# A 16-run, 8 KB load whose data nobody uses, issued ahead of the first load of a relu-and-mean kernel

## The chip, the cores and the metric

One Trainium2 chip, one of its cores. The metric is the device time of one execution in microseconds (us), as a median over the executions of a kernel. The profile's span (first to last instruction) is about 1.35 us shorter than the time of the same execution: 160.2 and 161.59 us for the profiled execution before.

## The reference

```python
x: (32, 512, 1024) float32
def reference(x):
    return np.mean(np.maximum(x, 0), axis=-1).astype(np.float32)   # (32, 512)
```

16,384 rows of 1,024 numbers are read, 67.1 MB, and 64 KB are written.

## The kernel before

128 rows (called the "row", because each of the 128 partitions, the parallel lanes of the on-chip buffer, gets one of them) are handled on their own; the other 16,256 rows lie on 128 partitions, 127 each, and are loaded 16 at a time (8 MB, 64 KB per partition) into three buffers. Rows are shared out between ScalarE (relu with a sum) and VectorE (max and add with a sum). The last 15 rows come in smaller pieces. All loads are issued by the sync engine (SP). Two of them, the row and the first big load, are moved ahead of the barrier at which all engines meet at the start of the program.

```python
NB, BUFS = 16, 3
def load(i, dst, src):
    nc.sync.dma_start(out=dst, in_=src).then_inc(loaded[i], 16)

for t in range(full):                      # full = 7
    buf_free(t)                            # from t = 3: waits for both compute engines
    if t == 0:
        load(-1, row0[:, :], xfirst)       # the row: 128 runs of 4 KB
    load(t, bufs[t % BUFS][:, :, :], xr[:, t * NB:(t + 1) * NB, :])   # big: 128 runs of 64 KB
    if t == BUFS:
        nc.sync.wait_ge(first, 2)
        nc.sync.dma_start(out=..., in_=turned0[0:P:32, :]).then_inc(stored, 16)   # the row's result
# ... smaller loads of the last 15 rows ...
# ... reductions, mostly hidden behind the loads ...
nc.sync.wait_ge(pool, 2)
nc.sync.wait_ge(dve, n_done + 2)
nc.sync.dma_start(out=outr, in_=res[:, :]).then_inc(stored, 16)       # the final store
nc.sync.sem_clear(range(used[0], used[-1] + 1))
nc.sync.wait_ge(stored, 32).then_inc(stored, -32)
# ...
issue_ahead_of_entry_barrier(nc, 2)        # the first two loads go in front of the barrier
```

## Time and profile before

| | before |
|---|---|
| time, median of 4 runs | 161.47 us (161.30 to 161.62) |
| span of the profiled execution | 160.2 us |
| DMA queue, share of 16 engines' span | 97.7% |
| VectorE, ScalarE busy | 46%, 44% |
| first packet on a DMA engine | 1.03 us |
| big loads on the engines from | 2.75 us |
| last data landed, final store issued | 157.82, 158.57 us |

The time is that of the DMA stream. The prediction below shows the lines; two things help in reading them. In a table of stretches a packet counts where it starts, so a stretch in which sixteen long packets start shows far more than the true rate and the next ones show zero. And the issue of a DMA (an SPq line of the timeline) is the time in which the sync engine prepares it, not the time in which data moves.

### The profile page before, as it was taken

How to read it: one execution, taken by the hardware profiler on the slowest of the kernel's cores; microseconds unless marked ns; L12 is line 12 of the kernel's file. 1: busy time of each engine (PE TensorE's matmuls, PEld its weight loads, DVE VectorE, ACT ScalarE, POOL GpSimd, SP SyncE). 2: the span in 40 equal slices, each digit the busy share in tenths (PEclk: the TensorE clock that was granted, in tenths of full speed). 3: DMA queues.
4: the chain of work that ended last, by engine and by line, in shares of the span. 5: the costliest groups of instructions: out<-in, count | busy, mean ns of one | idle time of the engine just before them, and what ended most of it. 6: DMA issues, size and time to landing. Idle time of an engine off the chain costs nothing. (4 is left out here: it accounts for less than half of the span.)

```text
span 160.2 us, 347 instructions
## 1 busy us (share of the span) xinstructions
DVE 73.3 (46%) x131; ACT 70.4 (44%) x133; POOL 1.3 (1%) x9
## 2 busy tenths in 40 slices
DVE  0000029900498006960079500993009920299984
ACT  1400029800496006950079300991009900299983
POOL 1000000000000000000000000000000000000001
DMA  9969969979989899699699699699699797998992
GB/s 393 507 278 523 507 278 523 442 344 523 409 376 523 360 425 524 294 491 523 262 524 523 262 523 524 262 523 523 262 524 458 327 523 327 425 451 367 419 412 102
DMA packets 2312, 67.18 MB, mean 419 GB/s; under 512 B 392, under 2 KB 648, under 8 KB 1032
## 3 DMA queue, kind: packets, MB, share of 16 engines
q1 hardware_dynamic: 2312, 67.18, 97.7%
HBM read 67.11 MB, written 0.07 MB: 419 GB/s over the span
## 5 line engine op out<-in xcount | busy, mean ns | idle before, releaser
L20 DVE TENSOR_SCALAR_CACHE_REDUCE rows<-rows 128x1024 f32<-128x1024 f32 (+1 forms) x63 | 72.1, 1208 | 78.9 <-DMA rows<-in_x_dram 78.7
L15 ACT ACTIVATE rows<-rows 128x1024 f32<-128x1024 f32 x64 | 66.2, 1035 | 84.1 <-DMA rows<-in_x_dram 83.9
L15 ACT ACTIVATION_READ_ACCUMULATOR rows<-rows 128x1 f32 x64 | 11.9, 186 | 0.0
L20 DVE DVE_READ_ACCUMULATOR rows<-rows 128x1 f32 x63 | 5.2, 82 | 0.0
L168 DVE STREAM_TRANSPOSE turned<-mean 128x32 f32<-128x32 f32 x1 | 0.2, 213 | 5.9 <-ACT row L164 5.9
L164 ACT ACT_TABLE_LOAD x1 | 1.3, 1283 | 3.3 <-DMA row<-in_x_dram 3.3
L157 POOL TENSOR_SCALAR res<-sums 128x112 f32<-128x112 f32 (+1 forms) x2 | 0.5, 250 | 154.0 <-DVE rows L20 154.0
L164 ACT ACTIVATE row<-row 128x1024 f32<-128x1024 f32 x1 | 1.1, 1056 | 0.0
L15 ACT ACTIVATE last<-last 128x512 f32<-128x512 f32 x1 | 0.6, 630 | 0.0
L20 DVE TENSOR_SCALAR_CACHE_REDUCE last<-last 128x256 f32<-128x256 f32 x1 | 0.4, 420 | 0.3 <-DMA last<-in_x_dram 0.3
L197 DVE SCALAR_TENSOR_TENSOR last<-last,scale 128x258 f32<-128x258 f32 x1 | 0.4, 428 | 0.1
L142 POOL MEMSET scale<- 128x258 f32 x1 | 0.3, 314 | 0.0
L187 POOL TENSOR_SCALAR res<-part 128x1 f32<-128x1 f32 x1 | 0.3, 267 | 0.6 <-DVE rows L20 0.6
L164 ACT ACTIVATION_READ_ACCUMULATOR row<-row 128x1 f32 x1 | 0.2, 186 | 0.0
L15 ACT ACTIVATION_READ_ACCUMULATOR last<-last 128x1 f32 x1 | 0.2, 186 | 0.0
L141 POOL MEMSET mean<- 128x32 f32 x1 | 0.1, 126 | 1.5 <-POOLq L55 1.5
L232 POOL MEMSET const-uint8-127<- 128x1 uint8 x1 | 0.1, 103 | 0.0
L232 POOL MEMSET const-bfloat16-1.0<- 128x1 bf16 x1 | 0.1, 102 | 0.0
L232 POOL MEMSET const-float32-0.0<- 128x1 f32 x1 | 0.1, 99 | 0.2 <-issue 0.2
L232 POOL MEMSET const-float32-1.0<- 128x1 f32 x1 | 0.1, 99 | 0.0
L20 DVE DVE_READ_ACCUMULATOR last<-last 128x1 f32 x1 | 0.1, 83 | 0.0
L197 DVE DVE_READ_ACCUMULATOR last<-last,scale 128x1 f32 x1 | 0.1, 82 | 0.0
## 6 DMA issues: line engine op xcount, KB each, us to landing
rows<-in_x_dram SPq DMA_DIRECT2D x1, 3584.0 KB, 38.1
rows<-in_x_dram SPq DMA_DIRECT2D x1, 2048.0 KB, 42.6
rows<-in_x_dram SPq DMA_DIRECT2D x1, 1024.0 KB, 44.7
row<-in_x_dram SPq DMA_DIRECT2D x1, 512.0 KB, 3.3
rows<-in_x_dram SPq DMA_DIRECT2D x1, 512.0 KB, 45.4
last<-in_x_dram SPq DMA_DIRECT2D x1, 256.0 KB, 45.6
last<-in_x_dram SPq DMA_DIRECT2D x2, 128.0 KB, 45.4
rows<-in_x_dram SPq DMA_DIRECT2D x7, 48.8
```

What stands on the lines that cost most here:

```text
L15: return nc.scalar.activation(out=src, in_=src, func=ACT.Relu, accum_out=acc)
L20: return nc.vector.tensor_scalar(out=src, in0=src, scalar1=0.0, scalar2=init, op0=ALU.max, op1=ALU.add, accum_out=acc,)
L141: nc.gpsimd.memset(mean0[:, :], 0.0)
L142: nc.gpsimd.memset(scale[:, :], inv).then_inc(pool, 1)
L157: nc.gpsimd.tensor_scalar(out=res[:, lo:hi], in0=sums[:, lo:hi], scalar1=inv, scalar2=0.0, op0=ALU.mult, op1=ALU.add,)
L164: nc.scalar.activation(out=row0[:, :], in_=row0[:, :], func=ACT.Relu, scale=inv, accum_out=mean0[:, 0:1],).then_inc(first, 1)
L168: nc.vector.transpose(turned0[:, :], mean0[:, :]).then_inc(first, 1)
L187: nc.gpsimd.tensor_scalar(out=res[:, J - 2:J - 1], in0=part[:, 0:1], scalar1=part[:, 1:2], scalar2=inv, op0=ALU.add, op1=ALU.mult,).then_i ...
L197: nc.vector.scalar_tensor_tensor(out=last[:, 768:], in0=last[:, 768:], scalar=0.0, in1=scale[:, :], op0=ALU.max, op1=ALU.mult, accum_out=r ...
L232: nc = _bacc.Bacc("TRN2", target_bir_lowering=False, num_devices=1)
```

## The change

The probe asks what one more transfer costs when it stands in front of everything else. Its data (16 runs of 512 B, one for each DMA engine) goes to a buffer that nobody reads. A semaphore tells that it has landed, and the sync engine waits for it much later, ahead of the fourth big load.

```diff
     first = nc.alloc_semaphore("first")
+    probe, probed = sbuf("probe", 16, 128), nc.alloc_semaphore("probed")
@@
     for t in range(full):
         buf_free(t)
+        if t == BUFS:
+            nc.sync.wait_ge(probed, 16)
         if t == 0:
+            nc.sync.dma_start(out=probe[:, :], in_=xfirst[0:P:8, :128]).then_inc(probed, 16)
             load(-1, row0[:, :], xfirst)
@@
-    used = [s.num for s in (*loaded, act, dve, pool, first)]
+    used = [s.num for s in (*loaded, act, dve, pool, first, probed)]
@@
-    issue_ahead_of_entry_barrier(nc, 2)
+    issue_ahead_of_entry_barrier(nc, 3)
```

## The prediction

> **What bounds the kernel now.** I read the page first (busy shares, the 40 slices, the DMA queue, the groups of instructions), then the two views of waits (the engines' and the sync queue's own), then the timeline of the sync queue, and last a table of stretches that I cut finely around the first and the last transfer, because the change touches only the first microseconds.
>
> The page:
>
> ```profile
> span 160.2 us, 347 instructions
> DVE 73.3 (46%) x131; ACT 70.4 (44%) x133; POOL 1.3 (1%) x9
> ...
> DMA  9969969979989899699699699699699797998992
> ...
> q1 hardware_dynamic: 2312, 67.18, 97.7%
> HBM read 67.11 MB, written 0.07 MB: 419 GB/s over the span
> ```
>
> Both compute engines are busy under half of the span, and the one DMA queue holds 97.7% of sixteen engines' time. So it is a stream of 67 MB with reductions hidden behind it.
>
> The views of waits, the engines' first and the sync queue's below it:
>
> ```profile
> ACT rows L15 <- DMA rows<-in_x_dram: 83.9, 9, 17.2
> DVE rows L20 <- DMA rows<-in_x_dram: 78.7, 8, 16.9
> ...
> SPq L115 <- DVE rows L20: 104.6, 5, 29.5
> ```
>
> The engines wait for data, never for each other in the main part. The 104.6 us of the sync queue look like the opposite, loads held up because buffers are not free; they are not a loss. The sync queue asks for the buffer of the first big load at 32.28 us, when the second load has still some ten microseconds to go (it lands 48.8 us after issue in the median of the page's issue list) and the third is queued behind it. Two loads are always ahead of the DMA engines.
>
> The table of stretches (columns: stretch and length; busy time of VectorE, ScalarE, GpSimd; clock; DMA share; GB/s):
>
> ```profile
> 0.50:1.00 0.50, 0.00 (x0) 0.00 (x0) 0.00 (x0) 1.00 0.00 0
> 1.00:1.20 0.20, 0.00 (x0) 0.00 (x0) 0.00 (x0) 1.00 1.20 123
> 1.20:1.40 0.20, 0.00 (x0) 0.00 (x0) 0.00 (x0) 1.00 1.19 205
> 1.40:1.60 0.20, 0.00 (x0) 0.00 (x0) 0.00 (x0) 1.00 0.00 0
> 1.60:1.70 0.10, 0.00 (x0) 0.00 (x0) 0.00 (x0) 1.00 1.19 492
> 1.70:2.20 0.50, 0.00 (x0) 0.00 (x0) 0.27 (x2) 1.00 1.04 410
> ...
> 2.70:22.00 19.30, 0.21 (x1) 2.43 (x3) 0.00 (x0) 1.00 1.01 435
> ...
> 157.20:157.40 0.20, 0.05 (x2) 0.20 (x1) 0.00 (x0) 1.00 0.17 51
> 157.40:158.57 1.17, 0.86 (x4) 0.49 (x2) 0.27 (x1) 1.00 0.00 0
> ```
>
> A packet is booked in the stretch where it starts, so zeros between 1.4 and 1.6 us mean that every DMA engine was inside its first packet, not that it idled. The reader should see three parts: about 1.03 us with no packet, a start-up in which each engine takes until about 1.65 us over one 4 KB packet (the raw packet records give 0.25 to 0.66 us for these, 0.159 us for each after them), then a gapless stream at about 435 GB/s until 157.4 us, and a fixed tail of 2.8 us (last reductions, the store, its landing). The end is therefore the moment at which the stream gets going, plus bytes over rate, plus the tail. A change moves the end only through one of these three.
>
> **What the Trainium skill says, and whether the trace agrees.** The page "DMA: Bandwidth & Descriptors", section "Latency and other measured facts", puts the first byte of a DMA issued by the sync queue at about 600 ns. Here the first packet starts 1.03 us after its issue begins, which is 0.64 us after the issue instruction ends (0.39 us); taken from the end of the issue the two agree. The store at the end shows 0.85 us from the start of the issue, 0.50 from its end.
>
> The same page, section "Queues, rings and completion order", says that on each DMA engine descriptors are consumed in ring order. So the row load's packets stand behind the probe's on the same engines. This trace agrees: the first load's packets all precede those of the second, and the small store that was issued at 32.66 us moves its packets only at 80.2 us, behind the loads that were queued before it.
>
> Its section "Why a DMA increments its semaphore by 16 and not by 1" says that a transfer is split over the largest number of engines up to 16 that divides its slowest dimension. For 16 partitions that is 16: one run of 512 B on each engine. No run shows that shape yet.
>
> "Perfetto Trace Analysis", section "DMA Instruction — HWDGE (DVE, Sync)", says that the slice of an issue covers the generation of descriptors and not the movement of data. The trace agrees: the first issue ends at 0.39 us and its data is moving from 1.03 us.
>
> **The change part by part.** It removes nothing. It adds one DMA issue at the head of the sync queue, 16 runs of 512 B, one more semaphore, one more wait on the sync queue before the fourth big load, and one more number in the clearing of semaphores. The order of instructions on the other engines is unchanged.
>
> The issue. The timeline of the sync queue:
>
> ```profile
> 0.00 0.39 SPq L109 DMA_DIRECT2D row<-in_x_dram  x1
> ...
> 32.66 0.63 SPq L125 DMA_DIRECT2D out_dram<-turned  x1
> ...
> 158.57 0.35 SPq L205 DMA_DIRECT2D out_dram<-res  x1
> ```
>
> The issue time hardly follows the number of runs: 0.39 us for 128 runs of 4 KB, 0.35 for 128 of 508 B, 0.63 for 4 runs of 128 B, 0.33 to 0.44 for the big loads. So I take 0.33 to 0.44 us for the probe and 0.05 us of gap (0.39 to 0.45 in the timeline): the row load's issue begins 0.38 to 0.49 us later, say 0.43.
>
> The bytes. 8 KB over 16 engines is one packet of 512 B each. Runs of 508 B took 0.027 us in the store, runs of 1 KB 0.046 us in the last loads, and a semaphore write 0.009 us. So 0.04 to 0.06 us of each engine's time.
>
> The wait before the fourth load. The probe has landed some 30 us earlier, so it costs one passed wait, about 0.02 to 0.05 us, in a place with about ten microseconds of slack: 0 on the path. The longer clearing lies beside the landing of the final store: 0. The barrier at entry moves by the 0.43 us, since the sync queue reaches it last (its drain begins at 0.93 us), and the third and fourth loads are issued that much later. They are queued behind a load that runs to 22 us: 0.
>
> What reaches the end is only the delay of the stream. If the row's data keeps its distance from its issue, that is 0.43 us. But the start-up of 0.25 to 0.66 us on the first packet looks partly like a cost of the first access; if the probe takes it, its packets being on the engines by 1.03 us as the row's were, the row could run from about 1.65 us as now, and only the 0.05 us of the bytes remains. I weigh 0.43 at 60%, something between (0.2 to 0.3) at 25% and 0.05 at 15%: 0.26 + 0.06 + 0.01 = about 0.33 us. 161.53 + 0.33 = about 161.85 us.
>
> **The rivals.** First, the warm-up in full. For it: the four earliest packets took 0.656 us each and the late starters 0.25 to 0.3, so all end within a short time of each other, as if one common event released them. Against it: that event can as well be the end of the row load's own descriptor generation or its own first read of memory, which come later with the row. The time would be 161.55 to 161.6.
>
> Second, the row's packets stall behind the probe: the engine finishes the probe's semaphore write, with its wait for the data to be confirmed, before it reads on. For it: small transfers pay a latency of their own (the row's landing is told 0.35 us after its last packet). Against it: at the seam between the row and the first big load the semaphore write lasts 0.009 us and the next packet starts 0.006 us after its start. The time would be 162.1 to 162.3.
>
> Third, the shift is absorbed by slack downstream. It can't be: with two loads queued at every moment, nothing later makes the DMA engines catch up; they already run at 435 GB/s.
>
> Fourth, the extra small transfer shifts the engines' phase and changes the rate. 1% of 155 us would be 1.5 us, but each engine gets the same extra run, so I give it 3%.
>
> **Range and chances.** The shift should be 0.05 to 0.5 us and the three times of the kernel before spread over 0.3 us, so a median is good to some 0.1 to 0.15. That gives 161.45 to 162.2 for 8 in 10. A change of 2% is 3.2 us, seven times the largest term; I leave 1% for each side: 1% faster, 98% within 2%, 1% slower.
>
> **What would show it.** In the changed profile the timeline of the sync queue should show the probe's issue at 0.00 with 0.33 to 0.44 us and the row's at about 0.43. The stretches should show 8 KB of packets near 1.03 us; the row's pipelined packets should start near 2.05 us if the shift is full, near 1.7 us if the start-up is absorbed, and the first reduction of a big load should move from 22.98 to 23.4 or 23.03 accordingly. The stream's rate and the tail should be as before. I am wrong if the first big load's landing moves by over 0.6 us, or not at all or to the left, or if the end moves by a different amount than that landing.

## The result, and the profile after

| | before | after |
|---|---|---|
| time, median of 4 runs | 161.47 us (161.30 to 161.62) | 162.09 us (162.07 to 162.33) |
| ratio after over before | | 1.0040, 95% interval 1.0025 to 1.0055 |

A ratio is the mean time of one kernel's runs over that of the other's of the same rounds, so it is not quite the ratio of the medians. Executions over 1.5% slower than the fastest of the same kernel are left out of the means. The medians are 0.62 us apart; the interval stands for 0.40 to 0.89 us. By the 2% measure the two are the same; the order of the two is clear of the noise.

The page after, its busy shares, DMA row and queue:

```profile
span 161.0 us, 348 instructions
DVE 73.3 (46%) x131; ACT 70.4 (44%) x133; POOL 1.3 (1%) x9
...
DMA  9899799699699699699699699699898998899992
...
q1 hardware_dynamic: 2344, 67.18, 97.4%
```

Nothing in the middle has changed: the same busy times, and the queue's 97.4% of 161.0 us is as much busy time as the 97.7% of 160.2 us before, within 0.3 us. The 32 packets more are 16 of data and 16 semaphore writes, one of each for every DMA engine, as the prediction had it.

The timeline of the sync queue after (start, length, both in us):

```profile
0.00 0.40 SPq L124 DMA_DIRECT2D probe<-in_x_dram  x1
...
0.45 0.41 SPq L110 DMA_DIRECT2D row<-in_x_dram  x1
0.90 0.43 SPq L110 DMA_DIRECT2D rows<-in_x_dram  x1
...
159.19 0.35 SPq L210 DMA_DIRECT2D out_dram<-res  x1
```

The probe takes one slot, 0.45 us, and the row and the big load are issued that much later. The final store's issue moves from 158.57 to 159.19 us, 0.62 us, more than the slot. The table of stretches after:

```profile
1.00:1.20 0.20, 0.00 (x0) 0.00 (x0) 0.00 (x0) 1.00 0.12 31
1.20:1.40 0.20, 0.00 (x0) 0.00 (x0) 0.00 (x0) 1.00 0.03 5
1.40:1.60 0.20, 0.00 (x0) 0.00 (x0) 0.00 (x0) 1.00 0.68 189
```

At 1.0 us, where the row's 4 KB packets started before (123 and 205 GB/s in the first two stretches), there is now only the 8 KB of the probe; its packets take 0.025 us each. The row's first packet starts at 1.48 us, 1.03 us after its issue, exactly the distance before. The long first packets come later as well: in the packet records, the row's packets of over 0.3 us end between 1.65 and 1.81 us before and between 2.05 and 2.17 us after. Then two waits, before and after, from the view of the engines' waits (total, times, longest):

```profile
ACT L164 <- DMA row<-in_x_dram: 3.3, 1, 3.3
```

```profile
ACT L169 <- DMA row<-in_x_dram: 3.7, 1, 3.7
```

The row lands about 0.4 us later (0.35 us by the semaphore records). The first big load follows; its first reduction, in the timelines before and after:

```profile
22.98 1.06 ACT L15 ACTIVATE rows<-rows 128x1024 f32<-128x1024 f32 x1 [17.19 <-DMA rows<-in_x_dram]
```

```profile
23.52 1.06 ACT L15 ACTIVATE rows<-rows 128x1024 f32<-128x1024 f32 x1 [17.38 <-DMA rows<-in_x_dram]
```

That is 0.54 us. One more wait has changed, the sync engine's own for its final store, before and after, from the sync queue's view of waits:

```profile
SPq L210 <- SPq L210: 1.2, 1, 1.2
```

```profile
SPq L215 <- SPq L215: 1.3, 1, 1.3
```

The raw semaphore records give this more finely: from the store's last packet to its last semaphore arrival it is 0.44 us before and 0.56 us after. Each of the sixteen DMA engines sends one arrival: the first seven come within 0.34 us before and 0.29 us after, the other nine between 0.39 and 0.44 us before and between 0.51 and 0.56 us after. So the profiled execution after is longer in two places: the last data lands 0.64 us later, and the store is confirmed 0.12 us later. Their sum of 0.76 us is the difference between the two profiled executions, 162.33 and 161.59 us, within 0.02.

### The profile page after: what moved, and what is told of

The parts are those of the page before. It is cut to its first block, busy times and chain, and to the rows that moved or that the text cites. A ratio compares the mean times of both kernels' runs of the same rounds, so it can differ in the third digit from the quotient of the medians.

```text
span 161.0 us, 348 instructions
## 1 busy us (share of the span) xinstructions
DVE 73.3 (46%) x131; ACT 70.4 (44%) x133; POOL 1.3 (1%) x9
## 3 DMA queue, kind: packets, MB, share of 16 engines
q1 hardware_dynamic: 2344, 67.18, 97.4%
```

## The experiments

All twelve give correct results. Each ran in five rounds (4 to 6 executions that count) beside the kernel before on the same chip; diffs are against the changed kernel and cut to the lines that matter (the size of the probe's buffer, for one, is left out). Theory I: the sync queue's issue slot ahead of the first data is what costs. Rival B: bytes, semaphore, wait or later barrier cost, wherever the probe stands.

This table has, for the profiled execution of each, when the row's last part landed, when the sixteen DMA engines started their first packet of the first big load, when the last data landed, and how long the final store took from its last packet to its last confirmation (all from the packet and semaphore records, in us). "Sum" is the shift of the last landing plus that of the confirmation, against before; "profiled" is the difference of the two profiled executions' times. The last two columns are the timed runs: difference of the medians of the same rounds, and the ratio with its interval.

| kernel | row landed | big load's first packets | last landing | confirmed | sum | profiled | medians | ratio |
|---|---|---|---|---|---|---|---|---|
| before | 3.28 | 2.75 to 2.92 | 157.82 | 0.44 | | | | |
| the change | 3.63 | 2.87 to 3.45 | 158.46 | 0.56 | 0.76 | 0.74 | 0.62 | 1.0040 (1.0025 to 1.0055) |
| e1 the change again | 3.80 | 3.09 to 3.49 | 158.25 | 0.56 | 0.55 | 0.53 | 0.53 | 1.0032 (1.0019 to 1.0046) |
| e12 4 runs ahead | 3.62 | 2.80 to 3.54 | 157.96 | 0.58 | 0.27 | 0.29 | 0.55 | 1.0030 (1.0016 to 1.0045) |
| e9 128 runs ahead | 3.67 | 3.04 to 3.43 | 158.21 | 0.91 | 0.86 | 0.83 | 1.03 | 1.0060 (1.0045 to 1.0075) |
| e4 two ahead | 4.15 | 3.50 to 3.80 | 158.89 | 1.19 | 1.81 | 1.80 | 1.29 | 1.0080 (1.0067 to 1.0094) |
| e8 a whole row ahead | 4.63 | 3.97 to 4.78 | 159.84 | 1.01 | 2.59 | 2.55 | 2.72 | 1.0152 (1.0129 to 1.0175) |
| e5 no probe | 3.21 | 2.36 to 3.16 | 157.62 | 0.45 | -0.19 | -0.21 | 0.06 | 1.0003 (0.9984 to 1.0022) |
| e6 behind the big load | 3.52 | 2.67 to 3.10 | 157.87 | 0.58 | 0.19 | 0.17 | 0.32 | 1.0013 (0.9996 to 1.0030) |
| e3 ScalarE's queue | 3.35 | 2.53 to 2.98 | 157.68 | 0.56 | -0.02 | -0.01 | 0.13 | 1.0017 (1.0004 to 1.0031) |
| e2 behind the row | 3.34 | 2.73 to 4.71 | 160.06 | 0.57 | 2.37 | 2.36 | 2.52 | 1.0158 (1.0144 to 1.0172) |
| e7 128 runs behind the row | 3.26 | 3.59 to 5.53 | 159.89 | 0.75 | 2.38 | 2.35 | 2.83 | 1.0173 (1.0147 to 1.0198) |
| e10 128 runs of 8 B behind | 3.26 | 2.69 to 5.28 | 160.02 | 0.87 | 2.62 | 2.59 | 2.80 | 1.0169 (1.0150 to 1.0188) |
| e11 as e7, big load later | 3.31 | 2.99 to 4.05 | 158.90 | 0.99 | 1.63 | 1.61 | 1.81 | 1.0108 (1.0092 to 1.0125) |

Two checks before the table is used. "Sum" and "profiled" agree within 0.04 us in every row, so the two terms are the whole account: nothing else in the program has changed its length. And single profiles of equal kernels differ: the last landing is 0.20 us earlier in e5 than before, where nothing should differ. The four kernels with one transfer ahead lie further apart, from 157.96 to 158.46 us. So some tenths of a microsecond of one last landing are noise, and means over several kernels or the timed runs must carry small claims. The profiles also come from different chips, and the one of the kernel before was taken apart from the experiments'; e5 to e8 share a chip and their rounds.

### e1: the change again

No edit.

> The changed kernel again, to narrow its cost. Theory I (the sync queue's issue slot): one issue plus gap is 0.45 us in the profile (0.00 to 0.45), so 0.40 to 0.50 us over before, ratio 1.0028. Theory L (landing): the row's packets also start later or slower behind the probe, as the last landing moved by 0.64 us in the one profile: 0.60 to 0.70 us, ratio 1.004.

Measured: ratio 1.0032, that is 0.52 us (0.31 to 0.74). With the first four runs (0.40 to 0.89) the cost lies near 0.55 to 0.6 us. Both intervals hold both expectations, so neither run decides between 0.45 and 0.62. Its profile does name the parts: 0.43 us in the last landing, 0.12 us in the confirmation of the store, again.

### e2: the probe second, behind the row

```diff
-            nc.sync.dma_start(out=probe[:, :], in_=xfirst[0:P:8, :128]).then_inc(probed, 16)
             load(-1, row0[:, :], xfirst)
+            nc.sync.dma_start(out=probe[:, :], in_=xfirst[0:P:8, :128]).then_inc(probed, 16)
```

> The same probe, issued second, after the row load. Same bytes, same number of issues, same barrier delay. Theory I: the row's stream starts at 1.03 us as before and runs to about 2.8 us, and the first big load, now issued at about 0.90 us, still has its packets ready before that, so only the probe's own 0.03 to 0.06 us remain: ratio 1.0000 to 1.0005. Rival B (the bytes, the extra semaphore, the wait before the fourth load or the later barrier cost the time, wherever the probe stands): +0.45 to 0.65 us, ratio 1.003 to 1.004.

Measured: 2.52 us over before. Neither theory had that; both fail here. The row itself is as before (landed at 3.34 us). The table of stretches, for the kernel before and for this one (the last number is GB/s of the packets that start in the stretch):

```profile
2.70:3.20 0.50, 0.00 (x0) 0.00 (x0) 0.00 (x0) 1.00 5.09 2130
3.20:3.80 0.60, 0.00 (x0) 0.45 (x1) 0.00 (x0) 1.00 0.00 0
3.80:4.40 0.60, 0.00 (x0) 0.60 (x1) 0.00 (x0) 1.00 0.00 0
4.40:5.00 0.60, 0.00 (x0) 0.59 (x2) 0.00 (x0) 1.00 0.00 0
```

```profile
2.70:3.20 0.50, 0.00 (x0) 0.00 (x0) 0.06 (x1) 1.00 4.78 1874
3.20:3.80 0.60, 0.00 (x0) 0.39 (x1) 0.00 (x0) 1.00 0.30 109
3.80:4.40 0.60, 0.00 (x0) 0.60 (x1) 0.00 (x0) 1.00 0.00 0
4.40:5.00 0.60, 0.00 (x0) 0.59 (x2) 0.00 (x0) 1.00 0.37 109
```

One 64 KB packet in 0.6 us is 109 GB/s. Before, all sixteen DMA engines start the big load together. Here fourteen do; one starts at 3.44 us and one at 4.71 us, and that packet then takes 3.54 us where 2.42 is usual. All engines carry equal shares, so this straggler is late to the end: the last landing is 2.24 us late, and the first reduction waits for it:

```profile
25.53 1.06 ACT L15 ACTIVATE rows<-rows 128x1024 f32<-128x1024 f32 x1 [19.67 <-DMA rows<-in_x_dram]
```

A share of the DMA engines averaged over 16 hides this; the latest of the 16 first packets shows it.

### e3: the probe on ScalarE's queue

```diff
-            nc.sync.dma_start(out=probe[:, :], in_=xfirst[0:P:8, :128]).then_inc(probed, 16)
+            nc.scalar.dma_start(out=probe[:, :], in_=xfirst[0:P:8, :128]).then_inc(probed, 16)
```

(The helper that moves loads ahead of the barrier accepts ScalarE's as well.)

> The probe is issued from ScalarE's queue, still before the entry barrier, so the sync queue's first instruction is the row load again. Theory I with a private issue slot: about 0 to 0.1 us over before. Theory I with descriptor generation shared between the two queues: the row's or the first big load's issue is stretched or held, +0.2 to 0.45 us if the probe gets in first, about 0.05 us if the row does. Rival B: +0.45 to 0.65 us.

Measured: 0.13 us by medians, 0.27 us (0.06 to 0.50) by the ratio. The head of the timeline:

```profile
0.00 0.39 SPq L110 DMA_DIRECT2D row<-in_x_dram  x1
0.12 0.38 ACTq L124 DMA_DIRECT2D probe<-in_x_dram  x1
```

The two issues overlap and the sync queue's has its usual length; the row lands at 3.35 us. The last landing is no later than before (157.68 us), and only the confirmation of the store is longer, by 0.12 us. (The interval of the times alone would not exclude 0.45 us; the profile does the work here.) So an issue on another queue, begun 0.12 us after the row's, doesn't hold the row up. It doesn't follow that the two queues prepare transfers independently. The probe lands much later after its issue than in the change, in the issue lists of the change and of this run (the last number is us from issue to landing):

```profile
probe<-in_x_dram SPq DMA_DIRECT2D x1, 8.0 KB, 1.7
```

```profile
probe<-in_x_dram ACTq DMA_DIRECT2D x1, 8.0 KB, 3.1
```

Its packets start at 2.19 to 2.63 us, 2.07 us or more after its issue began, while the row's have been moving since 1.02 us. Whether the preparation is shared and the row simply came first, or the DMA engines served the row's queue first, this run can't tell.

The Trainium skill, page "DMA: Bandwidth & Descriptors", section "Issuing engines are not separate DMA queues", says that starting DMAs on several engines saves only the sequencer's issue time, "usually small relative to the DMA itself". This trace agrees with the first half; at the head of the program that small time is on the path.

### e4: two probes ahead

```diff
+            nc.sync.dma_start(out=probe2[:, :], in_=xfirst[0:P:8, 128:256]).then_inc(probed, 16)
-            nc.sync.wait_ge(probed, 16)
+            nc.sync.wait_ge(probed, 32)
-    issue_ahead_of_entry_barrier(nc, 3)
+    issue_ahead_of_entry_barrier(nc, 4)
```

> Two probes of 16 runs of 512 B ahead of the row. Theory I: two slots, 0.85 to 0.95 us over before, ratio 1.0055. If the second costs less than the first (a start-up cost paid once, such as the widened spread of the engines): 1.05 to 1.1 us, that is 0.62 plus 0.45. If the cost is once only: 0.62 us.

Measured: 1.29 us (ratio 1.0067 to 1.0094, that is 1.08 to 1.52). The sync queue's timeline:

```profile
0.00 0.40 SPq L125 DMA_DIRECT2D probe<-in_x_dram  x1
0.46 0.40 SPq L126 DMA_DIRECT2D probe<-in_x_dram  x1
0.90 0.42 SPq L111 DMA_DIRECT2D row<-in_x_dram  x1
```

Two slots are 0.90 us, and the row lands 0.87 us later. The cost is per issue and not a start-up paid once. By medians the total is above all three expectations (the interval begins at 1.08 us, where the second one lies). In the profile the excess is in the final store: its wait is

```profile
SPq L217 <- SPq L217: 2.0, 1, 2.0
```

against 1.2 us before. That profiled execution was the longest of the five (163.39 against 162.66 to 162.82 us), so the wait was probably shorter in the others; no trace of them is kept.

### e5: no probe, only its semaphore and wait

```diff
-            nc.sync.dma_start(out=probe[:, :], in_=xfirst[0:P:8, :128]).then_inc(probed, 16)
-            nc.sync.wait_ge(probed, 16)
+            nc.sync.wait_ge(loaded[-1], 16)
-    issue_ahead_of_entry_barrier(nc, 3)
+    issue_ahead_of_entry_barrier(nc, 2)
```

> No probe; the extra semaphore, the longer clearing and a passed wait before the fourth big load stay. All theories that put the cost on the probe: 0 within 0.1 us. If the wait or the semaphore costs: part of the 0.53 to 0.62 us. It is also the control of how far two kernels that should be equal lie apart.

Measured: 161.44 against 161.38 us, ratio 1.0003 (-0.26 to 0.36 us). The wait, the semaphore and the longer clearing cost nothing that can be seen. The confirmation of the store takes 0.45 us, as before: the additional 0.12 us come with the probe's transfer. The row's first packets took 0.16 to 0.55 us here, 0.25 to 0.66 before, so their length varies between executions without any probe.

### e6: the probe third, behind the first big load

```diff
-            nc.sync.dma_start(out=probe[:, :], in_=xfirst[0:P:8, :128]).then_inc(probed, 16)
             load(-1, row0[:, :], xfirst)
         load(t, bufs[t % BUFS][:, :, :], xr[:, t * NB:(t + 1) * NB, :])
+        if t == 0:
+            nc.sync.dma_start(out=probe[:, :], in_=xfirst[0:P:8, :128]).then_inc(probed, 16)
```

> The same probe, third in the entry block, behind the row and the first big load. The barrier still comes 0.45 us later, the bytes and the wait are the same. Theory I (only the issue slot ahead of the first data counts): 0 to 0.1 us over before. Rival B (bytes, barrier, wait): 0.5 us. If the 2.5 us of the run with the probe second come from any small transfer between large ones on the same rings: again 2 us or more; if they come from descriptors of the first big load that reach one DMA engine late at the start: 0.

Measured: 0.21 us by the ratio (-0.06 to 0.48), 0.32 by medians. The barrier comes as late as in the change (the next load is issued at 2.40 us, against 1.93 before and 2.39 in the change), and the same bytes are moved, yet the last landing has not moved (157.87 us). Only the confirmation is longer, 0.58 us. So the later barrier and the bytes are ruled out as a cost of about 0.5 us, and a small transfer between two large ones doesn't make stragglers wherever it stands. The interval doesn't tell 0 from the 0.14 us of the confirmation.

### e7: behind the row, 128 runs

```diff
+            nc.sync.dma_start(out=probe[:, :], in_=xfirst[:, :128]).then_inc(probed, 16)   # behind the row
```

> The probe second, behind the row, but as 128 runs of 512 B, eight on each DMA engine. If the 2.5 us come from a transfer of one run per engine: gone, and 0.2 to 0.25 us from eight times 0.027 us of bytes. If they come from the first big load being the third transfer in quick succession (its descriptors late on one engine): the time over before stays at 1.5 to 2.5 us.

Measured: 2.83 us. Now all sixteen DMA engines are late: their first big packets start between 3.59 and 5.53 us, though the big load's issue ended at 1.34 us and the probe's data were through by about 3.3 us on most. One run per engine is not the cause. Of the two expectations the second held in direction, above its 1.5 to 2.5 us; but its reason, three transfers in quick succession, is not enough by itself (e9, below).

### e8: a whole second copy of the row ahead

```diff
+            nc.sync.dma_start(out=probe[:, :], in_=xfirst).then_inc(probed, 16)   # ahead, 128 runs of 4 KB
```

> Ahead of the row a probe of 128 runs of 4 KB: eight packets of 0.159 us on each engine, 1.27 us of bytes, more than the 0.45 us of an issue slot. Theory I in its full form (the stream starts at 1.03 us as before, and the row's issue is hidden behind the probe's data): 1.2 to 1.35 us over before, the bytes alone. If slot and bytes add up: 1.7 to 1.9 us. If the start-up of the first packets is paid twice: 1.7 us or more as well, and the row's first packets would again take 0.3 to 0.6 us.

Measured: 2.72 us by medians, 2.45 (2.08 to 2.82) by the ratio, more than any expectation. The row does what theory I says: it lands 1.35 us later, the bytes' 1.27 us and no slot on top. The rest comes from the big load's stragglers (first packets up to 4.78 us, over 0.4 us after the row was through on all sixteen engines; the last landing is 2.02 us late) and from the store's confirmation (1.01 us, 0.57 more). No transfer is small here, so stragglers don't need a small one.

### e9: 128 runs ahead

```diff
-            nc.sync.dma_start(out=probe[:, :], in_=xfirst[0:P:8, :128]).then_inc(probed, 16)
+            nc.sync.dma_start(out=probe[:, :], in_=xfirst[:, :128]).then_inc(probed, 16)
```

> The probe ahead of the row, as 128 runs of 512 B, eight times the bytes and packets. Theory I (the issue slot, with the bytes inside it: eight packets of 0.027 us are 0.22 us, less than the 0.45 us slot): the same as with 16 runs, 0.45 to 0.65 us over before. Bytes in addition to the slot: 0.75 to 0.85 us. If the late descriptors of the first big load (seen behind the row) come from three transfers in quick succession in any order: 2 us or more; if from descriptors still held when the big load is issued, the probe has drained by then and they are not seen.

Measured: 1.03 us by medians, 0.97 (0.73 to 1.21) by the ratio. That looks like a miss of theory I, and the parts tell why it isn't one at the head: the row lands at 3.67 us and the first reduction of the big load starts at 23.56 us, as with 16 runs (3.63 to 3.80 us, 23.52 and 23.57). Eight times the bytes are hidden in the slot. The row's long first packets are gone (none of the first sixteen took over 0.23 us), and the row lands no earlier for it. The store is confirmed after 0.91 us, 0.47 us more than before. There are no stragglers, though three transfers are issued as quickly as in e7: the order counts, not the number alone.

### e10: 128 runs of 8 B behind the row

```diff
+            nc.sync.dma_start(out=probe[:, :], in_=xfirst[:, :2]).then_inc(probed, 16)   # behind the row
```

> The probe second, behind the row, 128 runs of 8 B: as many descriptors as in the run with 128 runs of 512 B (2.8 us over before), a 64th of the bytes. If the number of descriptors that stand on the rings delays the first big load's: again 2 to 3 us. If the bytes or the traffic do: 0 to 0.3 us.

Measured: 2.80 us. One kilobyte in all, and again four engines start late, at 3.53, 3.57, 5.22 and 5.28 us. The bytes of the small transfer are not the cause. The number of descriptors alone isn't shown to be it either: with the same number, e7 had sixteen late engines.

### e11: as e7, with the big load issued after the barrier

```diff
-    issue_ahead_of_entry_barrier(nc, 3)
+    issue_ahead_of_entry_barrier(nc, 2)      # probe as in e7: 128 runs of 512 B, behind the row
```

> The probe second with 128 runs of 512 B, but the first big load is issued after the entry barrier, about 1.9 us instead of 0.91. If its descriptors wait until the row has drained from the rings (about 2.7 us): as late as before, 2 to 3 us over before. If the quick succession of three issues delays them: first packets at about 1.03 us after the issue, near 3.0 to 3.1 us, that is 0.2 to 0.5 us over before. If the later barrier matters little, either answer is clear.

Measured: 1.81 us, between the two expectations. The big load was issued a microsecond later than in e7 (1.93 instead of 0.91 us), and its first packets started earlier (2.99 to 4.05 instead of 3.59 to 5.53 us). The table of stretches, e7 and then e11 (in e7 no 64 KB packet of the big load starts in the first of them, in e11 nine do):

```profile
2.70:3.20 0.50, 0.00 (x0) 0.00 (x0) 0.07 (x1) 1.00 0.42 114
3.20:3.80 0.60, 0.00 (x0) 0.47 (x1) 0.00 (x0) 1.00 0.82 224
```

```profile
2.70:3.20 0.50, 0.00 (x0) 0.00 (x0) 0.00 (x0) 1.00 3.89 1309
3.20:3.80 0.60, 0.00 (x0) 0.42 (x1) 0.00 (x0) 1.00 1.28 437
```

A fixed distance from issue to first packet is out of the question, and so is one common moment that the row's end sets (its last packet ends at 2.91 us in e7 and at 2.96 in e11). Here the earlier issue, in quick succession behind transfers that still stood in the queue, made it worse; what in the hardware holds the engines back stays open.

### e12: 4 runs ahead

```diff
+            nc.sync.dma_start(out=probe[:, :], in_=xfirst[0:P:32, :128]).then_inc(probed, 16)
```

> The probe ahead of the row with 4 runs of 512 B: a quarter of the bytes, on 4 DMA engines. The store of 4 runs took 0.63 us to issue in every profile, against 0.33 to 0.45 of other transfers. Theory I: the slot of 4 runs is 0.65 to 0.70 us, so 0.20 to 0.25 us more than with 16 runs, 0.70 to 0.85 us over before, although less is moved. If bytes or packets set the cost: less than with 16 runs, 0 to 0.5 us. If this issue turns out to take 0.40 us, theory I says the same as with 16 runs.

Measured: 0.55 us by medians, 0.48 (0.26 to 0.73) by the ratio. The issue did not take the 0.63 us of the 4-run store:

```profile
0.00 0.37 SPq L124 DMA_DIRECT2D probe<-in_x_dram  x1
0.43 0.36 SPq L110 DMA_DIRECT2D row<-in_x_dram  x1
```

So the run doesn't vary the slot (0.43 us) and theory I says the same cost as with 16 runs, which is what came out with a quarter of the bytes. The profiled execution landed early (157.96 us), 0.26 us under the mean of the four kernels with one transfer ahead; its profile alone shows only 0.29 us of cost, so here the timed runs are the evidence.

No kernel here points to one that beats the kernel before. The best place for such a transfer is where e3 and e6 put it, off the sync queue or behind the first big load, and there it still costs up to the confirmation.

## Why the prediction was right or wrong

**The bound and the way a delay reaches the end: right.** The stream's rate and the reductions stayed, and what moved is its start and its tail. In all thirteen variants the shift of the last landing plus that of the confirmation is the whole difference.

**The issue slot of 0.38 to 0.49 us: right, and it reaches the end, in full as far as the noise tells.** It measured 0.45 us. The row's first packet kept its 1.03 us from the issue. With one slot ahead (the change, e1, e9, e12) the row landed at 3.68 us in the mean, with none (before, e2, e3, e5, e6, e7, e10, e11) at 3.31: 0.37 us. The last landing is 158.22 us in the mean of the same four against 157.75 of before, e3, e5 and e6: 0.47 us, with a standard error of about 0.12 us from their spread. The first big load's landing is steadier: 22.95 to 22.99 us in the same four without a slot, 23.32 to 23.54 us in the four with one, 0.51 us later in the mean. Two slots gave 0.84 us on the row and 1.1 us on the last landing (one profile).

**The weighing of that slot: the term that was mis-sized.** I gave the full shift only 60%, and made 0.33 us of 0.43. The warm-up rival, which took 40% of the weight with its in-between form, had only the long first packets for it, and e5 shows that these vary by themselves. Its absorption would have left the row near 3.3 us; it came at 3.6 to 3.8. And where the long first packets did vanish, in e9, the row landed at 3.67 us all the same. No run delayed the row's issue without a transfer, so that the slot's time costs, and not the mere presence of a transfer ahead, rests on e9 and e12 (the same cost with eight times and with a quarter of the bytes) and e4 (twice the slot).

**"The longer clearing lies beside the landing of the final store: 0", and a tail as before: wrong by 0.12 us.** The tail did not stay: the store's confirmation takes 0.44 and 0.45 us in the two profiles without a probe and 0.56 to 0.58 us in the six with one of 4 or 16 runs, wherever it stood and also from ScalarE's queue. I did not think of it, as nothing links a transfer of the first microsecond to a store at the end. The slot's 0.45 and these 0.12 make 0.57 us, which lies in the intervals of the change, e1 and e12. Why a store is confirmed later is not shown. It grew with the added transfers (0.75 to 1.01 us with 128 runs, 1.19 with two probes), but not in order of their size. The different chips aren't it: e5 (0.45 us) and e6 (0.58 us) ran on one chip, in the same rounds. And e5 has the extra semaphore too.

With that the prediction met one of its own signs of being wrong, "if the end moves by a different amount than that landing": in the profile after, the first big load's landing moved by 0.54 us and the end by 0.74. The path to the stream's start was right; that nothing else lies on the path was not.

**The rival of a stall behind the probe:** its time, 162.1 to 162.3 us, is near the measured one (162.09), but its mechanism is not what happened. The row's packets start 1.03 us after their own issue, on engines that had been through with the probe.

**The bytes, the wait, the barrier at no cost: right** (e9 at the head, e5, e6).

So the time fell into the stated range, 0.24 us above the predicted 161.85. About 0.12 us come from a shift taken at three quarters and 0.12 from the confirmation. The fit of that sum is partly luck: the base of 161.53 us was 0.06 above the median of 161.47 that the result has, so 0.05 of the 0.62 us between the medians remain, within the noise of the runs.

## What to carry to other kernels

In a kernel bound by its load stream, the first issue on the queue that feeds it is on the path: a transfer put ahead of it costs its whole issue slot (here 0.45 us, for 2 KB as for 64 KB; 512 KB cost more, its bytes), and the same transfer behind the first big load or on another queue leaves the landing of the data where it was. Don't put a small transfer between the first loads and the big one that they are meant to cover: here that cost 2.5 to 2.8 us, about six times the slot; why is open. When sixteen DMA engines share every load equally, look at the latest of them, not at the mean, and count the confirmation of the last store in the tail.

## What the Trainium skill lacked or had wrong

- "DMA: Bandwidth & Descriptors" gives the first-byte latency, but the issuing engine's own part of an issue only in cycles, in a comparison made for trn3, and no page gives it in time for this chip. It was 0.36 to 0.43 us plus about 0.05 us to the next in these profiles' first issues, hardly different for 4 runs of 512 B (0.37) and for 128 of 64 KB (0.43). Later issues differed more: 0.33 us for the next big load, 0.61 to 0.64 us for the 4-run store.
- The same page, section "Latency and other measured facts": its 0.6 us to the first byte fits only if it is counted from the end of the issue (0.64 us); from the start of the issue it was 1.03 us, for the row as the first transfer and as the second. The final store took 0.50 and 0.85 us.
- No page mentions that a large load issued right behind two others, the first of them large and still in the queue, starts late on some or all DMA engines: first packets up to 5.53 us after the start of the program instead of 2.92, cost 2.5 to 2.8 us (e2, e7, e10; e8 too has such late packets), less when it is issued later (e11).
- No page says that the confirmation of a final store can take longer when transfers were added long before it: 0.44 and 0.45 us after its last packet without the probe, 0.56 to 0.58 us with a small one, 0.75 to 1.19 us with larger ones or two.
